# The S5 branch's products and lower parts of the weights: from GpSimd to VectorE

## The chip, the core and the metric

The kernel runs on one core of a Trainium2 chip. The metric is the device time of one execution in microseconds, taken in several runs; the median is given with its range. A profile is one further execution with the hardware profiler on. In its rows PE is TensorE (PEld its weight loads), DVE is VectorE, ACT is ScalarE, POOL is GpSimd and SP is SyncE, which here only issues DMAs.

## What is computed

Two blocks in a row on 512 positions of width 1024: first a mixer of three branches with a squared-ReLU MLP, then a transformer-like layer with a gated delta rule, a Fourier mix and a mixture of experts. The change touches the first block's mixer, cut here to its parts:

```python
proj = jnp.einsum('bsd,de->bse', xn, w_in) + b_in
u_ssm, c_bgate, c_cgate, c_val, g_ssm, g_conv = jnp.split(proj, SPLIT_POINTS, axis=-1)
y_ssm = s5_branch(u_ssm, lam_re, lam_im, log_dt, b_re, b_im, c_re, c_im, d_skip)
z = jax.nn.gelu(y_ssm)
y_a = (z @ w_glu_a) * jax.nn.sigmoid(z @ w_glu_b)
y_b = (c_bgate * causal_short_conv(c_cgate * c_val, conv_w, conv_b)) @ w_conv_out
merged = jax.nn.sigmoid(g_ssm) * y_a + jax.nn.sigmoid(g_conv) * y_b
```

`s5_branch` is a diagonal state space model: 32 groups of 64 complex states, each a linear recurrence over the 512 positions, s[t] = a·s[t−1] + (B u)[t], and y = Re(C s) + d·u.

## The kernel before

**Matmuls in three passes.** Weights and activations are fp32; TensorE is fed a rounded form (fp32r), and each product is made of three: upper weight × upper activation, upper weight × lower activation, lower weight × upper activation. `weights` loads a 1024x256 piece of a weight by a DMA on SP's queue and cuts it into two chunks of 128 columns: ScalarE rounds a chunk to its upper part wh (L125), and the engine named by `self.lsub` subtracts to get the lower part wl (L126), each 128x1024, in two buffers each. `acc3` then runs 16 matmuls with wh (L130 and L131 in turn, the first two passes) and 8 with wl (L138, the third) into one of three PSUM tiles `acc`. `dense` walks over the chunks, hands each finished tile to a function that consumes it, and after each chunk lets the S5 branch go on by `fill` pieces.

**The S5 branch.** `s5` is a generator of 16 steps, each for 128 complex states (one per partition) over all 512 positions. A step has three pieces. First the phase: VectorE makes fr (L442, L445, L446), ScalarE sine sn, absolute value and cosine cs (L448 to L450), TensorE the two input products bu (L455). Then VectorE turns bu back by the phase (L460 to L465) and runs two real scans (L468, L469) that give zr and zi. Then the result is turned forward: sr = cs·zr − sn·zi and si = cs·zi + sn·zr. Here VectorE takes the products with cs (L473, L476), the difference (L475) and the sum (L478); GpSimd takes the two products with sn, n1 (L474) and n2 (L477). After every fourth step TensorE forms y from four sr and four si (L486), and VectorE, ScalarE and VectorE again make z and its two parts (L490, L491, L152, L153).

**The stage.** While S5 runs, TensorE works on 24 chunks of w_in for the convolution branch (its gates and values are consumed by VectorE and ScalarE at L541 to L557), 8 chunks of w_conv_out, and then 8 chunks of w_in for the gate of that branch (L571, L572). With `self.lsub = nc.gpsimd` in `block1` all these 40 chunks' lower parts are made on GpSimd. Behind the gate `lsub` is VectorE again, and z enters the next matmuls.

**What sets the order.** The instructions are laid out on each engine's queue by a scheduler when the program is built, from the order of the code and an estimate of durations. Each engine then takes its queue strictly in order and waits on semaphores, so what stands behind a waiting instruction waits as well.

Of the kernel before, what the change touches and what calls it, by code (L numbers as in the profile page):

```python
# [84 lines left out]
class Kern:  # L85
# [342 lines left out]

    def s5(self, sp, u, zH, zL):
        nc = self.nc  # L430
        V, G = nc.vector, nc.gpsimd
        S = [P, T]

        def t(tag, bufs=1):
            return sp.tile(S, F32, tag=tag, bufs=bufs, name=self.nm(tag))

        st = {}
        for j in range(16):

            fr = t("fr")  # L440
            n = t("m1")
            V.tensor_tensor(fr.rearrange("p (a b) -> p a b", b=16),  # L442
                            self.fa[:, j, :32].unsqueeze(2).broadcast_to([P, 32, 16]),
                            self.fa[:, j, 32:].unsqueeze(1).broadcast_to([P, 32, 16]), op=ALU.add)
            V.tensor_scalar(n, fr, MAGIC, MAGIC, op0=ALU.add, op1=ALU.subtract)  # L445
            V.tensor_sub(fr, fr, n)  # L446
            sn, cs = t("sn", 2), t("cs", 2)
            nc.scalar.activation(sn, fr, AF.Sin, scale=2 * math.pi * (1 - 2e-7))  # L448
            nc.scalar.activation(fr, fr, AF.Abs)
            nc.scalar.activation(cs, fr, AF.Sin, scale=-2 * math.pi, bias=self.halfpi)  # L450
            jr = slice(32 * (j % 4), 32 * (j % 4) + 32)
            bu = []
            for i in range(2):
                b = self.pp.tile(S, F32, tag="q", bufs=4, name=self.nm("bu"))
                nc.tensor.matmul(b, self.bbT[jr, i, j // 4], u[jr, j // 4], start=True, stop=True,  # L455
                                 tile_position=(32 * (j % 4), 0))
                bu.append(b)
            yield
            m1, m2, m3, m4 = t("m1"), t("m2"), t("m3"), t("m4")
            V.tensor_mul(m1, cs, bu[0])  # L460
            V.tensor_mul(m4, sn, bu[0])
            V.tensor_mul(m2, sn, bu[1])
            V.tensor_mul(m3, cs, bu[1])
            V.tensor_add(m1, m1, m2)
            V.tensor_sub(m3, m3, m4)  # L465
            zr, zi = m2, m4
            mg = self.mag[:, j:j + 1].broadcast_to(S)
            V.tensor_tensor_scan(zr, mg, m1, 0.0, op0=ALU.mult, op1=ALU.add)  # L468
            V.tensor_tensor_scan(zi, mg, m3, 0.0, op0=ALU.mult, op1=ALU.add)  # L469
            yield  # L470
            sr, si = t("sr", 4), t("si", 4)
            n1, n2 = m1, m3
            V.tensor_mul(sr, cs, zr)  # L473
            G.tensor_mul(n1, sn, zi)  # L474
            V.tensor_sub(sr, sr, n1)  # L475
            V.tensor_mul(si, cs, zi)  # L476
            G.tensor_mul(n2, sn, zr)  # L477
            V.tensor_add(si, si, n2)  # L478
            st[j % 4] = (sr, si)
            if j % 4 == 3:  # L480
                i4 = j // 4
                y = self.pp.tile(S, F32, tag="q", bufs=4, name=self.nm("y"))
                for i in range(2):
                    for a in range(4):
                        ja = slice(32 * a, 32 * a + 32)
                        nc.tensor.matmul(y[ja, :], self.ccT[:, i, i4, ja], st[a][i], start=(i == 0), stop=(i == 1),  # L486
                                         tile_position=(0, 32 * a), skip_group_check=True)
                ys = t("m1")
                z = t("m2")
                V.scalar_tensor_tensor(ys, u[:, i4], self.v["ssm_d"][:, i4:i4 + 1], y, op0=ALU.mult, op1=ALU.add)  # L490
                nc.scalar.activation(z, ys, AF.Gelu_apprx_tanh)  # L491
                self.split(z, zH[:, i4], zL[:, i4])
            yield

    def block1(self):
        nc, ins = self.nc, self.ins
        V, A = nc.vector, nc.scalar
# [24 lines left out]
        sp = self.pool("s5", es=es)  # L522
        zz = a2.tile([P, 2, 4, T], F32R, tag="Z", name="zz")
        zH, zL = zz[:, 0], zz[:, 1]
        self.lsub = nc.gpsimd
        self.fillers.append(self.s5(sp, u, zH, zL))

        cH = ap_.tile(B, F32R, tag="D", name="cH")
# [105 lines left out]
        zr = tp.tile([P, D], F32, name="zr")  # L634
# [1508 lines left out]
```

## Time and profile before

| | |
|---|---|
| time, median of 3 runs | 1989.0 us (1984.17 to 1991.39) |
| the profiled execution's own time | 1987.15 us |
| its span, first to last instruction | 1985.4 us |
| busy over the whole span: TensorE, VectorE, ScalarE, GpSimd | 1765.2, 1114.9, 585.3, 321.8 us |
| S5 steps, first phase sum to last S5 sum | 79 to 393 us |
| last third pass of the gate's chunks | 432 to 434 us |

The busy times are of the whole kernel, whose stages have different limits; they don't tell what this stage waits for. For that one reads the stretch from 79 to 395 us by itself: how full each engine is in it, which groups of instructions are long for their size, and what lies beside them on the other engines.

### The profile page before, as it was taken

How to read it: one execution, taken by the hardware profiler on the slowest of the kernel's cores; microseconds unless marked ns; L12 is line 12 of the kernel's file. 1: busy time of each engine (PE TensorE's matmuls, PEld its weight loads, DVE VectorE, ACT ScalarE, POOL GpSimd, SP SyncE). 2: the span in 40 equal slices, each digit the busy share in tenths (PEclk: the TensorE clock that was granted, in tenths of full speed). 3: DMA queues.
4: the chain of work that ended last, by engine and by line, in shares of the span. 5: the costliest groups of instructions: out<-in, count | busy, mean ns of one | idle time of the engine just before them, and what ended most of it. 6: DMA issues, size and time to landing. Idle time of an engine off the chain costs nothing. (4 is left out here: it accounts for less than half of the span.)

```text
span 1985.4 us, 24482 instructions
## 1 busy us (share of the span) xinstructions
PE 1765.2 (89%) x9169; PEld 1143.1 (58%) x9169; DVE 1114.9 (56%) x2231; ACT 585.3 (29%) x989; POOL 321.8 (16%) x210
## 2 busy tenths in 40 slices
PE   6778889699999999999998988999698898899985
PEld 4545556376676788777775665887333333333332
DVE  4889898833454665594466689573532323233225
ACT  3222324242343244332344633233411111111112
POOL 0434344420000000000012222003110111111000
PEclk9888889799999999999998889899799999999997
DMA  4111111138556333222231211006599999989993
GB/s 137 63 64 43 43 64 64 42 126 280 210 170 242 120 95 115 67 86 85 64 105 65 64 43 56 13 12 245 206 382 413 413 402 413 389 309 413 412 406 136
DMA packets 150266, 351.15 MB, mean 177 GB/s; under 512 B 20435, under 2 KB 107036, under 8 KB 130235
## 3 DMA queue, kind: packets, MB, share of 16 engines
q1 hardware_dynamic: 135533, 302.52, 41.2%
q0 software_dynamic: 9008, 33.58, 4.6%
q10 hardware_dynamic: 5534, 12.54, 1.7%
q8 instruction: 115, 1.88, 0.4%
q14 instruction: 76, 0.62, 0.1%
HBM read 339.63 MB, written 19.15 MB: 181 GB/s over the span
## 5 line engine op out<-in xcount | busy, mean ns | idle before, releaser
L125 ACT CAST wh<-w 128x1024 fp32r<-128x1024 f32 (+1 forms) x184 | 179.3, 975 | 407.7 <-PE acc L131 340.2
L126 POOL TENSOR_TENSOR wl<-w,wh 128x1024 fp32r<-128x1024 f32 (+1 forms) x76 | 184.7, 2434 | 621.0 <-PE acc L138 375.7
L1733 PE MATMUL gu<-ew,moe 128*64 128x512 f32 x1024 | 262.5, 639 | 14.2 <-DMA ew<-in_w_gate_dram 8.7
L126 DVE TENSOR_TENSOR wl<-w,wh 128x1024 fp32r<-128x1024 f32 (+1 forms) x108 | 123.2, 1141 | 118.7 <-PE acc L138 89.2
L1733 PEld LDWEIGHTS gu<-ew,moe 128*64 128x64 f32 x1024 | 73.9, 145 | 147.8 <-issue 120.4
L130 PE MATMUL acc<-xH,wh 128*128 128x512 f32 x352 | 151.3, 430 | 0.3 <-ACT wh L125 0.3
L131 PE MATMUL acc<-xL,wh 128*128 128x512 f32 x352 | 148.0, 420 | 0.0
L1742 DVE TENSOR_TENSOR moe<-gu,moe 64x512 f32<-64x512 f32 x32 | 21.8, 683 | 201.7 <-ACT moe L1741 136.2
L1758 PE MATMUL dn<-ew,hT 128*64 128x512 f32 x512 | 119.0, 608 | 0.5 <-ACT hT L1751 0.5
L130 PE MATMUL acc<-fH,wh 128*128 128x512 f32 x256 | 103.5, 405 | 0.4 <-ACT fH L152 0.4
L130 PE MATMUL acc<-gH,wh 128*128 128x512 f32 x256 | 103.2, 403 | 0.0
L1751 ACT COPY hT<-tr 128x128 f32<-128x128 f32 x64 | 13.9, 269 | 299.1 <-PE tr L1748 283.3
L131 PE MATMUL acc<-fL,wh 128*128 128x512 f32 x256 | 102.0, 398 | 0.0
L131 PE MATMUL acc<-gL,wh 128*128 128x512 f32 x256 | 102.0, 398 | 0.0
L138 PE MATMUL acc<-xH,wl 128*128 128x512 f32 x352 | 94.4, 412 | 6.5 <-DVE wl L126 3.7
L130 PEld LDWEIGHTS acc<-xH,wh 128*128 128x128 f32 x352 | 71.7, 204 | 42.3 <-issue 19.4
L1703 POOL DMA_INDIRECT yd<-moe,sx x31 | 32.0, 1033 | 339.2 <-DVE moe L1766 168.9
L131 PEld LDWEIGHTS acc<-xL,wh 128*128 128x128 f32 x352 | 71.5, 203 | 21.1 <-issue 5.5
L138 PEld LDWEIGHTS acc<-xH,wl 128*128 128x128 f32 x352 | 69.0, 197 | 24.0 <-DVE wl L126 4.2
L1758 PEld LDWEIGHTS dn<-ew,hT 128*64 128x64 f32 x512 | 36.4, 139 | 68.7 <-issue 63.8
L1766 DVE SCALAR_TENSOR_TENSOR moe<-dn,wv,moe 128x512 f32<-128x512 f32 x32 | 24.0, 751 | 89.5 <-PE dn L1758 64.6
L130 PE MATMUL acc<-hxH,wh 128*128 128x512 f32 x160 | 70.9, 447 | 2.1 <-DVE y L1248 2.1
(706 smaller groups left out, 3458.7 us busy)
## 6 DMA issues: line engine op xcount, KB each, us to landing
ew<-in_w_up_dram SPq DMA_DIRECT2D x64, 1024.0 KB
ew<-in_w_gate_dram SPq DMA_DIRECT2D x64, 1024.0 KB
ew<-in_w_down_dram SPq DMA_DIRECT2D x64, 1024.0 KB
w<-in_w_in_dram SPq DMA_DIRECT2D x36, 1024.0 KB
w<-in_w_ff_dram SPq DMA_DIRECT2D x32, 1024.0 KB
wm<-in_w_mod_dram POOLq DMA_DIRECT2D x24, 1024.0 KB, 6.5
xt<-in_x_dram SPq DMA_DIRECT2D x8, 512.0 KB
w<-in_w_conv_out_dram SPq DMA_DIRECT2D x4, 1024.0 KB
```

The lines of the kernel that those rows point to most:

```text
L125: nc.scalar.copy(H[:, :kt], W[:, :kt, c:c + P])
L126: self.lsub.tensor_sub(L[:, :kt], W[:, :kt, c:c + P], f(H[:, :kt]))
L130: self.nc.tensor.matmul(ps, H[:, k], aH[:, k, sl], start=(k == 0), stop=False)
L131: self.nc.tensor.matmul(ps, H[:, k], aL[:, k, sl], start=False, stop=False)
L138: nc.tensor.matmul(ps, L[:, k], aH[:, k, sl], start=False, stop=(k == kt - 1))
L1703: nc.gpsimd.indirect_dma_start(out=self.yd.rearrange("r (m c) -> (r m) c", m=m), out_offset=bass.IndirectOffsetOnAxis(ap=sx, axis=0), in_= ...
L1733: mm = M.matmul(gu[64 * j:64 * j + 64], xs[:, k, s0:s0 + 64], ws[2 * (k // 4) + j][:, k % 4], start=(n == 0), stop=(n == 7), tile_position ...
L1742: V.tensor_mul(gh[:64], gu[:64], gh[64:])
L1751: put(hT[:, q:q + 2], pt[:, 64 * q:64 * q + 128].rearrange("p (k s) -> p k s", k=2))
L1758: M.matmul(dn[64 * j:64 * j + 64], hT[:, q], ws[4 + q // 2][:, q % 2, 512 * j:512 * j + 512], start=(q == 0), stop=(q == 3), tile_position ...
L1766: V.scalar_tensor_tensor(y, dn, wsl, m5, op0=ALU.mult, op1=ALU.mult)
```

## The change

Three edits. In `s5` the two products with sn go to VectorE (`V` in place of `G`). In `block1` the line that sets `self.lsub` to GpSimd for the S5 stage is gone, so that it stays VectorE, as `setup` set it. Since one line is missing, all lines from 525 on are one lower in the program of after (L549 of before is L548 of after).

```diff
 def s5(self, sp, u, zH, zL):
     nc = self.nc
-    V, G = nc.vector, nc.gpsimd
+    V = nc.vector
...
     V.tensor_mul(sr, cs, zr)
-    G.tensor_mul(n1, sn, zi)
+    V.tensor_mul(n1, sn, zi)
     V.tensor_sub(sr, sr, n1)
     V.tensor_mul(si, cs, zi)
-    G.tensor_mul(n2, sn, zr)
+    V.tensor_mul(n2, sn, zr)
     V.tensor_add(si, si, n2)
...
 sp = self.pool("s5", es=es)
 zz = a2.tile([P, 2, 4, T], F32R, tag="Z", name="zz")
 zH, zL = zz[:, 0], zz[:, 1]
-self.lsub = nc.gpsimd
 self.fillers.append(self.s5(sp, u, zH, zL))
```

The scheduler then lays out the queues anew, from the S5 preparation to the end of the gate; the rows of the later stages stand in the order they had. Three places, with tiles named by the program (m is the tag of the step's four work tiles; the numbers tell instances apart).

VectorE, the tenth S5 step, from the phase to the first products with sine and cosine. Before:

```order
L442 TENSOR_TENSOR fr_1470<-fa 128x512
L445 TENSOR_SCALAR m_263_1471<-fr_1470 128x512
L446 TENSOR_TENSOR fr_1470<-fr_1470,m_263_1471 128x512
L462 TENSOR_TENSOR m_273_1519<-sn_1475,bu_1482 128x512
L460 TENSOR_TENSOR m_272_1518<-cs_1476,bu_1480 128x512
```

The same place after:

```order
L445 TENSOR_SCALAR m_263_1471<-fr_1470 128x512
L556 SCALAR_TENSOR_TENSOR cc_1458<-acc_1534,vt,cc_1458 128x512
L446 TENSOR_TENSOR fr_1470<-fr_1470,m_263_1471 128x512
L126 TENSOR_TENSOR wl_1573<-w_1570,wh_1572 128x1024
L462 TENSOR_TENSOR m_273_1519<-sn_1475,bu_1482 128x512
L153 TENSOR_TENSOR cL<-cc_1458,cH 128x512
L126 TENSOR_TENSOR wl_1630<-w_1570,wh_1629 128x1024
L460 TENSOR_TENSOR m_272_1518<-cs_1476,bu_1480 128x512
```

Two lower parts, which stood on GpSimd's queue, now stand between the phase and the product with the cosine.

VectorE, the end of the same step, where sr and si are formed. Before:

```order
L473 TENSOR_TENSOR sr_1562<-cs_1476,m_273_1519 128x512
L476 TENSOR_TENSOR si_1563<-cs_1476,m_275_1521 128x512
L475 TENSOR_TENSOR sr_1562<-sr_1562,m_272_1518 128x512
L478 TENSOR_TENSOR si_1563<-si_1563,m_274_1520 128x512
L442 TENSOR_TENSOR fr_1603<-fa 128x512
```

The same place after:

```order
L473 TENSOR_TENSOR sr_1562<-cs_1476,m_273_1519 128x512
L474 TENSOR_TENSOR m_272_1518<-sn_1475,m_275_1521 128x512
L476 TENSOR_TENSOR si_1563<-cs_1476,m_275_1521 128x512
L475 TENSOR_TENSOR sr_1562<-sr_1562,m_272_1518 128x512
L477 TENSOR_TENSOR m_274_1520<-sn_1475,m_273_1519 128x512
L442 TENSOR_TENSOR fr_1603<-fa 128x512
L478 TENSOR_TENSOR si_1563<-si_1563,m_274_1520 128x512
```

The products n1 (L474) and n2 (L477) stand among the others, and the next step's phase sum (L442) is drawn ahead of the last sum.

TensorE, the two chunks 1251 and 1304 of one load, at the third pass of the first. Before:

```order
L138 MATMUL acc_1251<-xH,wl_1248 128x512 x8
L455 MATMUL bu_1296<-u,bbT 128x512
L455 MATMUL bu_1298<-u,bbT 128x512
L130 MATMUL acc_1304<-xH,wh_1300 128x512
L131 MATMUL acc_1304<-xL,wh_1300 128x512
```

The third passes of the same two chunks after:

```order
L130 MATMUL acc_1304<-xH,wh_1300 128x512
L131 MATMUL acc_1304<-xL,wh_1300 128x512
L138 MATMUL acc_1251<-xH,wl_1248 128x512 x8
L138 MATMUL acc_1304<-xH,wl_1301 128x512 x8
L486 MATMUL y_1351<-sr_1077,ccT 32x512
L486 MATMUL y_1351<-sr_1145,ccT 32x512
```

The first chunk's third pass moved behind all the matmuls with the second chunk's upper part, so that both third passes stand together.

## Rows read from the trace of the kernel before

**Rows 1.** The page's first line: span and instructions.

```profile
span 1985.4 us, 24482 instructions
```

**Rows 2.** Busy time by stretch: stretch, length, PE, PEld, DVE, ACT, POOL, PEclk, DMA, GB/s.

```profile
79.00:395.00 316.00, 254.21 (x882) 163.11 (x880) 284.16 (x296) 89.43 (x118) 137.49 (x64) 0.86 0.16 54
395.00:434.00 39.00, 39.00 (x162) 31.37 (x163) 13.53 (x10) 17.22 (x20) 14.10 (x8) 0.97 0.30 109
434.00:560.00 126.00, 125.07 (x600) 86.28 (x599) 49.16 (x73) 42.30 (x61) 8.40 (x15) 1.00 0.66 234
```

**Rows 3.** VectorE's groups, 79 to 395 us: busy us, mean ns | idle before.

```profile
L478 DVE TENSOR_TENSOR si<-si,m 128x512 f32<-128x512 f32 x16 | 39.1, 2442 | 0.0
L475 DVE TENSOR_TENSOR sr<-sr,m 128x512 f32<-128x512 f32 x16 | 28.2, 1760 | 1.2 <-POOL m L474 1.2
L476 DVE TENSOR_TENSOR si<-cs,m 128x512 f32<-128x512 f32 x16 | 27.2, 1701 | 0.0
...
L460 DVE TENSOR_TENSOR m<-cs,bu 128x512 f32<-128x512 f32 x16 | 10.9, 683 | 9.4 <-ACT cs L450 9.3
```

**Rows 4.** VectorE's timeline: start us, duration us, instruction, [idle before].

```profile
99.86 0.41 DVE L445 TENSOR_SCALAR m<-fr 128x512 f32<-128x512 f32 x1
100.19 0.54 DVE L549 TENSOR_SCALAR cc<-vp,vt 128x512 f32<-128x512 f32 x1
100.65 0.68 DVE L446 TENSOR_TENSOR fr<-fr,m 128x512 f32<-128x512 f32 x1
101.25 0.74 DVE L550 SCALAR_TENSOR_TENSOR cc<-vp,vt,cc 128x512 f32<-128x512 f32 x1
101.92 0.74 DVE L547 SCALAR_TENSOR_TENSOR vp<-acc,vt,cg 128x512 f32<-128x512 f32 x1
...
106.83 1.21 DVE L468 TENSOR_TENSOR_SCAN m<-magk,m 128x512 f32<-128x512 f32 x1
107.97 1.19 DVE L469 TENSOR_TENSOR_SCAN m<-magk,m 128x512 f32<-128x512 f32 x1
...
313.80 0.68 DVE L478 TENSOR_TENSOR si<-si,m 128x512 f32<-128x512 f32 x1
```

**Rows 5.** GpSimd's timeline, one S5 step, and where it idled later.

```profile
129.44 1.53 POOL L474 TENSOR_TENSOR m<-sn,m 128x512 f32<-128x512 f32 x1 [11.14 <-DVE m L469]
130.94 1.70 POOL L477 TENSOR_TENSOR m<-sn,m 128x512 f32<-128x512 f32 x1
132.60 2.78 POOL L126 TENSOR_TENSOR wl<-w,wh 128x1024 fp32r<-128x1024 f32 x1
...
320.23 5.34 POOL L126 TENSOR_TENSOR wl<-w,wh 128x1024 fp32r<-128x1024 f32 x2 [6.90 <-ACT m L491]
```

**Rows 6.** VectorE's timeline beside the same step.

```profile
129.77 1.75 DVE L476 TENSOR_TENSOR si<-cs,m 128x512 f32<-128x512 f32 x1
131.44 1.74 DVE L475 TENSOR_TENSOR sr<-sr,m 128x512 f32<-128x512 f32 x1
133.11 2.82 DVE L478 TENSOR_TENSOR si<-si,m 128x512 f32<-128x512 f32 x1
135.86 0.68 DVE L153 TENSOR_TENSOR cL<-cc,cH 128x512 fp32r<-128x512 f32 x1
```

**Rows 7.** VectorE's timeline at a lower part that it makes itself.

```profile
41.03 1.22 DVE L126 TENSOR_TENSOR wl<-w,wh 128x1024 fp32r<-128x1024 f32 x1
42.17 0.17 DVE L207 SCALAR_TENSOR_TENSOR dt<-dt,er 128x16 f32<-128x16 f32 x1
```

**Rows 8.** Waits of TensorE, 60 to 430 us: total us, times, longest.

```profile
PE y L486 <- DVE sr L475: 27.2, 7, 7.6
...
PE acc L138 <- POOL wl L126: 2.7, 1, 2.7
```

**Rows 9.** TensorE's timeline in the gate: third passes of two chunks.

```profile
403.89 2.03 PE L138 MATMUL acc<-xH,wl 128*128 128x512 f32 x8
...
409.51 2.03 PE L138 MATMUL acc<-xH,wl 128*128 128x512 f32 x8
```

## The prediction

> **What bounds the kernel now.** I read the stretches first, then the groups of one engine, then the timeline of two engines side by side, and last the waits. The S5 steps run from 79 us (first phase sum, L442) to about 393 us (last L478). Between 79 and 395 us VectorE is busy 284.16 of 316 us, TensorE 254.21 at a granted clock of 0.86 of full speed (a mix of the two levels 1.2 and 2.4 GHz), GpSimd 137.49 with 64 instructions, ScalarE 89.43 [rows 2]. So VectorE is the fullest engine and idles only 316 − 284 = 32 us; 9.4 us of that are waits for the cosine of the step [rows 3].
>
> But VectorE's busy time isn't all its own work. The groups L476, L475 and L478 have means of 1.70, 1.76 and 2.44 us for 128x512 elements, while L460, of the same size but with one of its inputs in PSUM, takes 0.68 us in the mean of its sixteen [rows 3]. The timelines say why: GpSimd runs n1, n2 and a lower part wl back to back from 129.44 to 135.38 us [rows 5], and each VectorE instruction that lies beside it ends just after the GpSimd instruction that started before it: si (L476) runs until 131.52, sr (L475) until 133.18, si (L478) until 135.93. With GpSimd done, the next sum takes 0.68 us again [rows 6]. In a step in which GpSimd then idled, from 313.3 to 320.2 us, L478 took 0.68 us too, at 313.80 [rows 4, 5]. The two engines take turns here, and what GpSimd does costs VectorE nearly as much time as it costs GpSimd.
>
> Behind VectorE stands TensorE: it waited 27.2 us for sr before the y products, and only 2.7 us for a lower part from GpSimd [rows 8]. From 395 us on the last seven chunks of the gate run with TensorE busy 39.00 of 39 us, and so it stays until 560 us (125.07 of 126) [rows 2]: what the S5 stretch gains, TensorE starts earlier by, and nothing in that stage holds it.
>
> **The change, part by part.** Clean prices, from start to start of rows that follow each other without a gap [rows 4]: a 128x512 sum or product 0.60 us, a one-input form (L445, L549) 0.33 to 0.46, a fused form (L550) 0.67, a scan (L468) 1.14. A 128x1024 lower part on VectorE takes 1.14 us, from 41.03 to 42.17 us [rows 7].
>
> *Removed: the turns.* In the stretch VectorE has 296 instructions [rows 2]. By kind, counted in the program: 204 sums, products and splits at 0.60 = 122.4; 16 + 8 one-input forms = 9.0; 32 scans = 36.5; 35 fused forms = 23.5; one copy. Together 191 us. It was busy 284, so 93 us are stretching. Three groups carry most of it: 27.2 + 28.2 + 39.1 − 48 × 0.60 = 65.7 us [rows 3]. With no arithmetic on GpSimd all 93 us go.
>
> *Added to VectorE.* 32 products × 0.60 = 19.2 us, and the 30 lower parts that now stand between the first phase sum and the last L478: 30 × 1.14 = 34.2 us. Sum 53.4 us. VectorE's work in the stretch becomes 191 + 53 = 244 us, 40 less than its 284.
>
> *The idle time of VectorE.* Before, 32 us. Two things move it. In most steps the lower parts now stand between the phase (L446) and the first uses of sine and cosine (L462, L460), so they fill some of those 9.4 us. Against that, a lower part waits in VectorE's queue for its upper part from ScalarE, and for TensorE's third pass to free the buffer of two chunks before; behind it stand the S5 products and with them y on TensorE. Before, GpSimd could wait there alone. That wait has no row of its own: its bounds are 9 us less (the cosine waits all covered) and 30 us more (1 us for each of the 30). I take it as cancelling and keep 32 us, since the filled waits are rows and the new ones fall where ScalarE is busy only 89 of 316 us. Stretch: 244 + 32 = 276 us, 40 less than 316.
>
> *TensorE as the next.* It has 254 us of busy time in the stretch at clock 0.86, so 276 leaves it 22 us of idle time where it had 62. At full speed a chunk takes 5.62 us (403.89 to 409.51 us, third pass to third pass) [rows 9]; the 31 chunks of the stretch need 174 us of it, so part of the 254 is the lower clock after waits, and some comes back. TensorE's order changes too: the third passes of two chunks now stand together behind both chunks' first passes, which gives a late lower part some 4 us more before TensorE waits for it.
>
> *After the stretch.* The last y products stand one chunk earlier in TensorE's order: half a third pass and seven whole chunks follow, where before nine matmuls, one third pass and six chunks followed. That is about 2.5 us more behind the last S5 step, and as much less before it, when TensorE isn't last: +2 us. VectorE's eight lower parts there cost 1.14 us in a cycle of 5.62 and are hidden by TensorE. *Before the stretch* four lower parts move from GpSimd: between −4 × (2.78 − 1.14) = −6.6 and +4 × 1.14 = +4.6 us; I take −1, since GpSimd's stretch the preparation in the same way. *GpSimd's queue:* the DMAs of the modulation weights no longer stand behind lower parts and may start earlier, with DMA at 0.16 of its capacity in the stretch [rows 2]: 0.
>
> Sum: −40 + 2 − 1 = −39, say −40 us. The profiled execution took 1987.15 us, 1.75 more than its span of 1985.4 [rows 1], and lies 1.85 below the median of 1989.0. 1987 − 40 = **1947 us**.
>
> **A rule that speaks against it.** VectorE is busy 0.90 of the stretch and GpSimd 0.44 [rows 2]. The Trainium skill, "Perfetto Trace Analysis", section "Optimizing Scalar/DVE Operations", says that where VectorE is saturated it may make sense to hand some work to GpSimd; the change does the opposite. The same passage adds that the two share a read port of SBUF, so that moving work between them might not help. By the first half the time would be that of rival C, by the second that of the sum; rows 5 and 6 show the turns, so I go by the second.
>
> **The rivals.**
> *A, TensorE holds the stretch back.* If TensorE keeps its 254 us at clock 0.86 and half or more of its 62 us of waits, because y still stands behind sr and si in its order, the stretch is 285 to 301 us, the gain 15 to 31 and the time 1956 to 1972. For it: VectorE's work (244) is now below TensorE's busy time (254). Against: the waits for sr shrink with VectorE, and the clock rises when waits go.
> *B, the waits shrink too.* If the lower parts cover the cosine waits and TensorE is always ahead, VectorE idles 12 to 20 us: stretch 256 to 264, time 1927 to 1935. For it: the places of the lower parts in the order. Against: TensorE would have to run nearly without a wait.
> *C, slower.* If the long L475, L476 and L478 were not due to GpSimd, VectorE would keep its 284 us and get 53 more: stretch 337 + 32 = 369, time 2040. It decides from 53 us of stretching that stays, of the 93. Against: L478 at 0.68 us where GpSimd was idle [rows 4, 5].
> *D, given back later.* If the modulation weights or a later stage started at a fixed time, the gain would be lost behind 434 us and the time 1980 to 1990. Against: TensorE is full there [rows 2], and the order of the program behind the gate is unchanged.
> That the change doesn't do what it says is out: the new program has no arithmetic on GpSimd between the S5 preparation and the modulation.
>
> **How the numbers follow.** The forecast with idle time between 22 and 42 us, 1937 to 1957: 0.50. A beyond it, up to 1972: 0.25. B, 1927 to 1937: 0.14. C: 0.04. D: 0.05. Anything else: 0.02. The range takes in the forecast and most of A and B: 1930 to 1970, about 0.82. A measurement of this kernel can tell about 0.5% (10 us) from no change: faster 0.90 (forecast, A, B and a little), same 0.06, slower 0.04.
>
> **What would show it.** L475, L476 and L478 at 0.68 us in all sixteen steps, n1 and n2 at 0.68 and lower parts at about 1.2 us on VectorE; VectorE busy about 244 us from the first L442 to the last L478, and that stretch 270 to 285 us long; TensorE's waits for sr below 27 us and a clock over 0.86. Wrong would be: VectorE's instructions still stretched (C); VectorE idle over 50 us with waits for TensorE (A); the gate beginning 40 us earlier and the end not (D).

## The result: faster, by half as much again as forecast

The changed kernel takes 1929.54 us in the median of 4 runs (1923.76 to 1932.94), the kernel before 1990.2 on the same chip: a ratio of 0.9693, 95% interval 0.9654 to 0.9732. A second measurement beside other runs gave 1927.88 (0.9689, 0.9661 to 0.9716). The gain is 61 us where 40 were forecast, and the time lies just outside the stated range of 1930 to 1970. The profiled execution of the changed kernel took 1923.76 us, 1921.9 of it span; it was the shortest of its runs.

Busy time of the changed kernel by stretch, in the columns of [rows 2] (stretch, length, PE, PEld, DVE, ACT, POOL, PEclk, DMA, GB/s): the S5 steps, the rest of the gate, and as much behind it as the third row of [rows 2] has:

```profile
77.00:336.00 259.00, 233.00 (x859) 154.63 (x858) 245.35 (x357) 87.37 (x114) 0.00 (x0) 0.93 0.18 61
336.00:378.00 42.00, 42.00 (x178) 32.88 (x177) 14.08 (x19) 18.56 (x23) 2.01 (x3) 1.00 0.37 127
378.00:504.00 126.00, 124.37 (x597) 85.79 (x596) 49.14 (x73) 41.78 (x61) 8.39 (x15) 1.00 0.66 232
```

The first row of [rows 2] ends 2 us behind the last S5 sum. Cut there, the S5 steps of the kernel before are:

```profile
79.00:393.00 314.00, 252.27 (x879) 162.83 (x877) 283.55 (x296) 89.43 (x118) 137.49 (x64) 0.87 0.17 54
```

The S5 steps last 259 us where they lasted 314. Of these 55 us, VectorE is busy 38 less, though it executes 61 instructions more, and it idles 17 less: 259 − 245 = 14 us where it idled 314 − 284 = 30. TensorE is full again from there on, as in [rows 2]. VectorE's groups in the first stretch, in the columns of [rows 3]:

```profile
L126 DVE TENSOR_TENSOR wl<-w,wh 128x1024 fp32r<-128x1024 f32 x30 | 36.4, 1216 | 1.2 <-PE acc L138 1.2
...
L460 DVE TENSOR_TENSOR m<-cs,bu 128x512 f32<-128x512 f32 x16 | 10.9, 683 | 3.2 <-ACT cs L450 3.1
L462 DVE TENSOR_TENSOR m<-sn,bu 128x512 f32<-128x512 f32 x16 | 10.9, 682 | 2.1 <-ACT sn L448 2.1
...
L476 DVE TENSOR_TENSOR si<-cs,m 128x512 f32<-128x512 f32 x16 | 10.9, 682 | 0.0
...
L475 DVE TENSOR_TENSOR sr<-sr,m 128x512 f32<-128x512 f32 x16 | 10.9, 681 | 0.0
L478 DVE TENSOR_TENSOR si<-si,m 128x512 f32<-128x512 f32 x16 | 10.9, 681 | 0.0
```

The three long groups of [rows 3] are at 0.68 us. The wait for the cosine at L460 has gone from 9.4 to 3.2 us. Its neighbour, the wait for the sine, stood one row further in the same view of the kernel before:

```profile
L462 DVE TENSOR_TENSOR m<-sn,bu 128x512 f32<-128x512 f32 x16 | 10.9, 683 | 6.8 <-ACT sn L448 5.9 <-PE acc L131 0.7
```

Why these waits shrank is seen in VectorE's timeline of the changed kernel (start us, duration us, instruction):

```profile
126.68 0.68 DVE L446 TENSOR_TENSOR fr<-fr,m 128x512 f32<-128x512 f32 x1
127.28 1.22 DVE L126 TENSOR_TENSOR wl<-w,wh 128x1024 fp32r<-128x1024 f32 x1
128.45 0.69 DVE L462 TENSOR_TENSOR m<-sn,bu 128x512 f32<-128x512 f32 x1
129.06 1.22 DVE L126 TENSOR_TENSOR wl<-w,wh 128x1024 fp32r<-128x1024 f32 x1
130.32 0.69 DVE L460 TENSOR_TENSOR m<-cs,bu 128x512 f32<-128x512 f32 x1
```

From the end of the phase (L446) ScalarE needs some microseconds for sine, absolute value and cosine. Two lower parts now lie in that time, and VectorE goes from one product to the next without a pause. Twelve of the sixteen steps have one or two lower parts there, 17 of the 30 in all. Of the 5.3 us of waits that are left, 2.8 are those of the first step, which has none.

One reading of the forecast turned round: TensorE no longer waits much for sr, but it waits for lower parts. Its waits from 60 to 375 us in the changed kernel (total us, times, longest), against 27.2 and 2.7 us in [rows 8]:

```profile
PE acc L138 <- DVE wl L126: 19.2, 5, 8.8
PE y L486 <- DVE sr L475: 5.5, 3, 4.7
```

What these waits cost by themselves isn't shown. It is TensorE that ends the stage: it is busy without a pause from the last S5 sum to the gate's last third pass. From the first phase sum to there, before and after:

```profile
79.00:434.00 355.00, 293.21 (x1043) 194.47 (x1042) 297.69 (x306) 106.65 (x138) 151.59 (x72) 0.88 0.18 60
77.00:378.00 301.00, 275.00 (x1036) 187.51 (x1035) 259.44 (x375) 105.92 (x136) 2.01 (x3) 0.94 0.21 70
```

Its matmuls are nearly the same (1043 and 1036 records). The 54 us are 36 us less idle time of TensorE (62 to 26) and 18 us less busy time, at a mean granted clock of 0.94 in place of 0.88 (mixes of its two levels, 1.2 and 2.4 GHz). The shorter chain on VectorE pays by what TensorE no longer waits for.

### The profile page after: what moved, and what is told of

The parts are those of the page before. It is cut to its first block, busy times and chain, and to the rows that moved or that the text cites. A ratio compares the mean times of both kernels' runs of the same rounds, so it can differ in the third digit from the quotient of the medians.

```text
span 1921.9 us, 24414 instructions
## 1 busy us (share of the span) xinstructions
PE 1746.7 (91%) x9169; PEld 1134.6 (59%) x9169; DVE 1074.8 (56%) x2303; ACT 585.9 (30%) x988; POOL 162.5 (8%) x138
## 5 line engine op out<-in xcount | busy, mean ns | idle before, releaser
L126 DVE TENSOR_TENSOR wl<-w,wh 128x1024 fp32r<-128x1024 f32 (+1 forms) x148 | 171.8, 1162 | 139.7 <-PE acc L138 100.9
L130 PE MATMUL acc<-xH,wh 128*128 128x512 f32 x352 | 145.0, 412 | 0.0
L131 PE MATMUL acc<-xL,wh 128*128 128x512 f32 x352 | 141.7, 402 | 0.0
L138 PE MATMUL acc<-xH,wl 128*128 128x512 f32 x352 | 101.1, 435 | 23.8 <-DVE wl L126 23.8
L126 POOL TENSOR_TENSOR wl<-w,wh 128x1024 fp32r<-128x1024 f32 (+1 forms) x36 | 78.5, 2185 | 456.6 <-PE acc L138 308.9
L130 PE MATMUL acc<-fH,wh 128*128 128x512 f32 x256 | 103.7, 406 | 0.4 <-ACT fH L152 0.4
L130 PE MATMUL acc<-gH,wh 128*128 128x512 f32 x256 | 103.2, 403 | 0.0
L138 PEld LDWEIGHTS acc<-xH,wl 128*128 128x128 f32 x352 | 72.9, 211 | 48.0 <-DVE wl L126 28.2
L130 PEld LDWEIGHTS acc<-xH,wh 128*128 128x128 f32 x352 | 67.7, 192 | 35.3 <-issue 12.0
L131 PEld LDWEIGHTS acc<-xL,wh 128*128 128x128 f32 x352 | 67.5, 192 | 17.8 <-issue 3.2
L130 PE MATMUL acc<-hxH,wh 128*128 128x512 f32 x160 | 71.6, 452 | 2.1 <-DVE y L1247 2.1
L131 PE MATMUL acc<-hxL,wh 128*128 128x512 f32 x160 | 68.6, 433 | 0.0
```

The lines of the kernel that those rows point to most:

```text
L126: self.lsub.tensor_sub(L[:, :kt], W[:, :kt, c:c + P], f(H[:, :kt]))
L130: self.nc.tensor.matmul(ps, H[:, k], aH[:, k, sl], start=(k == 0), stop=False)
L131: self.nc.tensor.matmul(ps, H[:, k], aL[:, k, sl], start=False, stop=False)
L138: nc.tensor.matmul(ps, L[:, k], aH[:, k, sl], start=False, stop=(k == kt - 1))
```

## The experiments

The theory of the forecast is that VectorE and GpSimd take turns, so that GpSimd's work costs VectorE most of its length. For the idle time, which fell by 17 us where the forecast kept it, there are two theories: **1**, the lower parts on VectorE's queue fill the waits for sine and cosine; **2**, the turns themselves made the idle time. In the runs "the gate's end" is the first matmul with z (L130 with zz; L137 in e6), at 433.9 us in the kernel before and 377.7 in the changed one. Ratios are to the kernel before on the same chip. The edits of e1 and e2 stand against the kernel before, that of e8 and e9 is the same on either kernel, and the others stand against the changed kernel.

### Only the products (e1)

```diff
-            G.tensor_mul(n1, sn, zi)
+            V.tensor_mul(n1, sn, zi)
...
-            G.tensor_mul(n2, sn, zr)
+            V.tensor_mul(n2, sn, zr)
```

> Only the two products of each S5 step go to VectorE; the lower parts stay on GpSimd. Both theories take VectorE's work from 191 us (all clean) to 191 + 19 = 210, plus turns with the 32 lower parts, 85.6 of GpSimd's 137.5 us, so about 58 of the 93 us of stretching: 268 us from the first phase sum to the last S5 sum. Theory 1 (the lower parts on VectorE's queue fill its waits for sine and cosine, which is why its idle time fell from 30 to 14 us): none stand there in this kernel, the waits for sine and cosine stay at 15 us, the idle time about 30, the stretch 298, the time 1990 - 16 = 1974. Theory 2 (the turns themselves made the idle time, products and lower parts alike): idle about 20 us, stretch 288, time 1964.

Measured: 1957.83 us, ratio 0.9827 (0.981 to 0.9843). The S5 steps last 299 us, the length of theory 1, but in part by luck: VectorE is busy 260 us where 268 were expected, and idles 39 where 30 were:

```profile
81.00:380.00 299.00, 265.02 (x960) 175.29 (x958) 259.87 (x331) 101.09 (x128) 99.75 (x35) 0.92 0.19 62
```

and VectorE's groups in it have the two waits whole:

```profile
L462 DVE TENSOR_TENSOR m<-sn,bu 128x512 f32<-128x512 f32 x16 | 10.9, 684 | 11.8 <-ACT sn L448 11.6
L460 DVE TENSOR_TENSOR m<-cs,bu 128x512 f32<-128x512 f32 x16 | 10.9, 683 | 17.6 <-ACT cs L450 17.5
```

They are 29 us, more than the 15 expected and than the kernel before had. They did not shrink with the products' turns, and theory 2, which had an idle time of 20 us, is out. What made them longer is in part ScalarE's queue. In the last step the sigmoid of a gate chunk (L571) stands there between sine and cosine, with loads of function tables of 1.28 us each, and VectorE waits twice:

```profile
362.48 0.69 DVE L462 TENSOR_TENSOR m<-sn,bu 128x512 f32<-128x512 f32 x1 [3.65 <-ACT sn L448]
368.18 0.69 DVE L460 TENSOR_TENSOR m<-cs,bu 128x512 f32<-128x512 f32 x1 [3.02 <-ACT cs L450]
```

But the time is 16 us below theory 1's: the new order draws some three chunks of the gate into the stretch (960 matmul records where [rows 2] has 882), and the gate ends 22 us after the last S5 step where the kernel before needed 41. A stretch is thus not the time; the gate's end, here 401.4 us, is.

### Only the lower parts (e2)

```diff
-        self.lsub = nc.gpsimd
```

> Only the lower parts go to VectorE; the two products of each step stay on GpSimd. VectorE's work: 191 + 30 x 1.14 = 225 us, plus turns with the 32 products, 53 of GpSimd's 137.5 us, so about 36 us: 261. Theory 1 (the lower parts fill the waits for sine and cosine): these waits fall to about 5 us as in the changed kernel, idle time about 14 us, stretch 275, time 1990 - 39 = 1951. Theory 2 (the turns made the idle time): idle about 24 us, stretch 285, time 1961.

Measured: 1954.24 us, ratio 0.982 (0.9802 to 0.9838). The S5 steps last 277.7 us, near theory 1's 275, and the gate ends at 401.3. The length alone doesn't decide between the theories, since VectorE is busy 8 us less than expected and idles 24 us, which is theory 2's figure:

```profile
77.00:354.00 277.00, 233.07 (x844) 154.60 (x847) 252.75 (x323) 86.78 (x113) 52.57 (x32) 0.92 0.17 57
```

The waits decide. VectorE's groups from 77 to 354 us:

```profile
L475 DVE TENSOR_TENSOR sr<-sr,m 128x512 f32<-128x512 f32 x16 | 27.0, 1688 | 7.1 <-POOL m L474 7.1
L476 DVE TENSOR_TENSOR si<-cs,m 128x512 f32<-128x512 f32 x16 | 21.9, 1366 | 0.0
L460 DVE TENSOR_TENSOR m<-cs,bu 128x512 f32<-128x512 f32 x16 | 10.9, 683 | 3.2 <-ACT cs L450 2.9
L462 DVE TENSOR_TENSOR m<-sn,bu 128x512 f32<-128x512 f32 x16 | 10.9, 679 | 2.1 <-ACT sn L448 2.1
```

With lower parts in VectorE's queue the waits for sine and cosine are 5 us, with the turns of the products still there (L475, L476), as theory 1 has it. The rest of the 24 us are other waits: 7 us for GpSimd's products (L475), and some 12 for TensorE and at the lower parts. Each half of the change moves the gate's end by 32.5 us, both together by 56. The halves don't add up. TensorE's idle time up to the gate's end, 62 us before and 26 in the changed kernel, is 34 us with the products alone and 44 with the lower parts alone; why the two overlap isn't shown.

### The products once more, for nobody (e3)

```diff
             V.tensor_add(si, si, n2)
+            g1, g2 = t("g1"), t("g2")
+            nc.gpsimd.tensor_mul(g1, sn, zi)
+            nc.gpsimd.tensor_mul(g2, sn, zr)
```

> The changed kernel, and GpSimd takes the two products of each step once more into tiles that nobody reads (32 products, about 52 us of GpSimd). Theory of the turns: VectorE's instructions beside them are stretched by about 0.68 of that, 35 us, and the time is about 1930 + 35 = 1965, though nobody waits for GpSimd. Rival (the long instructions before came from waiting for GpSimd's results or buffers, not from its work): no change, 1930, all VectorE means as in the changed kernel.

Measured: 1963.75 us, ratio 0.9861 (0.9839 to 0.9883): 34 us above the first measurement of the changed kernel, as the turns would have it. No engine waits for these products in the trace, yet two of VectorE's groups are long again (from 76 to 368 us):

```profile
L474 DVE TENSOR_TENSOR m<-sn,m 128x512 f32<-128x512 f32 x16 | 28.2, 1765 | 0.0
L473 DVE TENSOR_TENSOR sr<-cs,m 128x512 f32<-128x512 f32 x16 | 26.7, 1669 | 0.0
```

GpSimd's 32 products take 59 us, and VectorE's busy time is 279.3 us, 34 more than in the changed kernel. This shows the mechanism by itself: it needs no wait for a result or a buffer of GpSimd's.

### Zeros in place of products (e4)

```diff
+        g1 = sp.tile([P, D], F32, name="g1")
+        for _ in range(240):
+            nc.gpsimd.memset(g1, 0.0)
         self.fillers.append(self.s5(sp, u, zH, zL))
```

> The changed kernel, and GpSimd writes zeros into one tile without a pause, 240 times 128x1024, some 230 us from the start of the S5 steps on. Theory (VectorE and GpSimd take turns only where GpSimd reads): no change, 1930, VectorE's two-input instructions at 0.68 us. Rival (any arithmetic instruction of GpSimd makes VectorE wait): VectorE is stretched by some 0.68 x 230 = 156 us, time about 2086.

Measured: 1933.54 us, ratio 0.9702 (0.9683 to 0.972), with GpSimd busy 231 of the 263 us of the S5 steps. VectorE's groups in them (L551 is the first tap of the convolution, L548 in the changed kernel):

```profile
L475 DVE TENSOR_TENSOR sr<-sr,m 128x512 f32<-128x512 f32 x16 | 10.9, 681 | 0.0
L478 DVE TENSOR_TENSOR si<-si,m 128x512 f32<-128x512 f32 x16 | 10.9, 680 | 0.0
L445 DVE TENSOR_SCALAR m<-fr 128x512 f32<-128x512 f32 x16 | 10.7, 672 | 0.0
L551 DVE TENSOR_SCALAR cc<-vp,vt 128x512 f32<-128x512 f32 x8 | 8.1, 1017 | 0.0
```

The instructions with two tensors don't feel a GpSimd that only writes. The two one-input forms do: 0.67 and 1.02 us in the mean, where the changed kernel has 0.42 and 0.54. Together that is 10.7 + 8.1 − 6.7 − 4.3 = 7.8 us. The Trainium skill, "SBUF — State Buffer", section "Who interferes with whom", says the same: a VectorE instruction with two inputs in SBUF contends with a GpSimd instruction that reads SBUF and not with one that only writes it, while one-input forms can enter a mode that takes both of VectorE's ports and contends with GpSimd. This run agrees with the part on writes (two-input instructions at 0.68 us), and with the last part in that the one-input forms grew longer; which mode they were in it doesn't show.

### The changed kernel again (e5)

The kernel is the changed one, without an edit.

> The changed kernel once more, on the chip of the runs beside it. Time 1930; the gate's last third pass at 378 us as in the first profile. If the 5 us that the profile gained behind the gate belong to the change, the stretch from the gate's end to the first gather of the experts is 985 us again and the rest 559; if they are chance, both move by some microseconds.

Measured: 1927.88 us. The gate ends at 375.3 us, 2.4 earlier than in the first profile; from there to the first gather of the experts it takes 989.0 us (985.1 in the first profile of this kernel, 987.2 in the kernel before), and from the gather to the end 563.9 (559.1 and 564.3). Behind the gate the first profile had gained 7 us of the 63.5 between the two spans; here the same program loses 1 us there. So those 7 us are not shown to be the change's; the 56 to 59 us at the gate's end are.

### No lower parts at all (e6)

The weights' own lower parts of the S5 stage are left out; all third passes take one lower part that is made once.

```diff
+            nc.scalar.copy(H[:, :kt], W[:, :kt, c:c + P])
+            if self.nolow:
+                if self.L0 is None:
+                    self.L0 = self.a2.tile([P, 8, P], F32R, tag="L0", name="L0")
+                    self.lsub.tensor_sub(self.L0, W[:, :, c:c + P], f(H))
+                yield H, self.L0
+                continue
             L = self.wp.tile([P, 8, P], F32R, tag="wl", bufs=2, name=self.nm("wl"))
-            nc.scalar.copy(H[:, :kt], W[:, :kt, c:c + P])
...
+        self.nolow = True
         self.fillers.append(self.s5(sp, u, zH, zL))
...
         self.lsub = nc.vector
+        self.nolow = False
```

> The changed kernel without the lower parts of the S5 stage: the third passes all take one lower part, made once (the weights' own lower parts of 39 chunks are left out, the matmuls are all there). VectorE's work falls by 30 x 1.14 to 211 us. Theory 1 (the lower parts on VectorE's queue fill the waits for sine and cosine): with none there these waits grow from 5 us to 15 or more. Theory 2 (the waits shrank because GpSimd's turns went): they stay at 5 us. The S5 part then ends with TensorE, whose busy time of 233 us is the floor: stretch 235 to 245 us, time 1910 to 1920.

Measured: 1897.16 us, ratio 0.9535 (0.9509 to 0.9562), 31 us below the changed kernel on the same chip and more than expected. VectorE's groups from 75 to 321 us, where L467 and L469 are the lines L460 and L462:

```profile
L467 DVE TENSOR_TENSOR m<-cs,bu 128x512 f32<-128x512 f32 x16 | 11.0, 687 | 12.2 <-ACT cs L457 12.1
L469 DVE TENSOR_TENSOR m<-sn,bu 128x512 f32<-128x512 f32 x16 | 11.0, 685 | 8.6 <-ACT sn L455 8.5
```

With no lower parts there, and nothing on GpSimd either, the waits for sine and cosine are 21 us again: theory 1 is shown from the other side. TensorE is then the fuller engine (238.57 of 246 us, at a clock of 0.98), so VectorE has little more to give there. The 31 us, 26 of them at the gate's end (349.0 us), are what making the lower parts on VectorE still costs, TensorE's waits for them included.

### The second block's lower parts (e7 and e11)

```diff
-        self.lsub = Q
```

> The changed kernel, and the 36 lower parts of the second block's x path (L126 on GpSimd, 78.5 us there) go to VectorE too. Theory of the turns: VectorE's work there rises by 20 x 1.14 + 16 x 0.60 = 32 us and falls by up to 0.68 x 78 = 53; VectorE is fullest from 1100 to 1200 us (0.91). Gain 0 to 15 us, time 1915 to 1930. Rival: VectorE's queue then holds back the matmuls, which wait there for it: 5 to 15 us slower.

Measured: 1922.21 us, ratio 0.9654 (0.962 to 0.9687). The same kernel once more:

> The kernel of e7 again, in more rounds: 1922 if its 6 us below the changed kernel were real, 1929 if they were chance.

Measured: 1924.57 us, ratio 0.9658 (0.9638 to 0.9679). Both lie 3 to 6 us below the changed kernel, but the intervals overlap with its 0.9661 to 0.9716: likely a small gain, not settled. From the gate's end to the first gather the two profiles take 981.6 and 978.9 us, where the changed kernel took 985.1 and 989.0, which speaks for the gain. The turns are there too: the costliest group of VectorE between 1100 and 1200 us (a fused form) takes 0.91 us in the mean in e5 and 0.74 in e7. What limits that stage along its length wasn't tested.

### The phase one step ahead (e8 and e9)

The same edit on both kernels: the phase (L442 to L450) becomes a function that is called for the next step behind the scans' inputs, with its scratch n in a tile of its own.

```diff
-        for j in range(16):
-
+        def phase(j):
             fr = t("fr")
-            n = t("m1")
+            n = t("n")
...
+            return sn, cs
+
+        ph = phase(0)
+        for j in range(16):
+            sn, cs = ph
...
             V.tensor_sub(m3, m3, m4)
+            if j < 15:
+                ph = phase(j + 1)
             zr, zi = m2, m4
```

On the kernel before:

> The kernel before, all of GpSimd's work in place, but each step's phase (L442 to L450) is made one step ahead, behind the scans, so that sine and cosine are ready. If VectorE's waits for sine and cosine (15 us of its 30 us of idle time) are time on the path, the stretch falls from 314 to about 299 us and the time to 1975. If they only cover waits that come anyway (for TensorE, or GpSimd's turns), the time stays at 1990.

Measured: 1969.76 us, ratio 0.9908 (0.9879 to 0.9936), 20 us faster with GpSimd's work as it was. The waits for sine and cosine fell from 15 to 3 us, the S5 steps from 314 to 289, the gate's end to 415.2. From 80 to 369 us:

```profile
80.00:369.00 289.00, 232.79 (x841) 154.18 (x843) 273.99 (x294) 88.09 (x115) 136.21 (x63) 0.89 0.17 55
```

So there were two ways to shorten those waits: other work in the gap, as the change did, or the phase earlier. But they make up 12 of the 25 us only. VectorE is also busy 9 us less, with as much work on GpSimd: the new order changed what lies beside it. That the waits alone were worth 20 us isn't shown. In VectorE's groups of that run the waits are (L466 and L464 are the lines L462 and L460):

```profile
L466 DVE TENSOR_TENSOR m<-sn,bu 128x512 f32<-128x512 f32 x16 | 10.8, 676 | 2.0 <-ACT sn L447 2.0
...
L464 DVE TENSOR_TENSOR m<-cs,bu 128x512 f32<-128x512 f32 x16 | 10.8, 674 | 3.5 <-PE bu L459 2.8 <-ACT cs L449 0.7
```

On the changed kernel:

> The changed kernel with each step's phase made one step ahead. In the kernel before that was worth 20 us. If what it gave there were the waits for sine and cosine, only 5 us of them are left here: time 1930 - 5 = 1925. If it helps TensorE as well (y and the input products earlier), up to 15 us more. If it costs, because the phase displaces the scans on VectorE's queue, the time is above 1930.

Measured: 1941.11 us, ratio 0.9762 (0.9736 to 0.9788), 12 to 13 us slower than the changed kernel. The gain that the expectation put first, 5 us, had the wrong sign; it allowed for a cost, but by another cause. The waits for sine and cosine are 3 us, but VectorE now waits longer for TensorE, which has done less by then in the new order of the queues. From 77 to 340 us:

```profile
L562 DVE SCALAR_TENSOR_TENSOR cc<-acc,vt,cc 128x512 f32<-128x512 f32 x8 | 5.9, 742 | 4.4 <-PE acc L138 4.4
L552 DVE SCALAR_TENSOR_TENSOR vp<-acc,vt,cg 128x512 f32<-128x512 f32 x8 | 5.9, 739 | 4.3 <-PE acc L138 4.3
L496 DVE SCALAR_TENSOR_TENSOR m<-u,vt,y 128x512 f32<-128x512 f32 x3 | 2.2, 747 | 5.1 <-PE y L492 5.1
```

and more of the gate is left behind the last S5 step: 821 matmul records lie in the S5 steps in place of 860, and from the last S5 sum it takes 48 us in place of 42, the gate's end at 388.0.

### Put together (e10 and e12)

> The changed kernel with the phase one step ahead, no lower parts on GpSimd in the second block either, and the first tap of the convolution (8 instructions of 0.46 us) on ScalarE. Gains if they add up: 5 us, 6 us (as e7 measured) and 4 us: time 1930 - 15 = 1915, about 75 us below the kernel before. If the schedule of the new order eats the small ones, 1922 as e7 alone.

Measured: 1924.58 us, ratio 0.9683 (0.9655 to 0.9711): 3 to 5 us below the changed kernel, within the noise, where 15 were expected. The edits are the phase ahead, that of e7 and the first tap of the convolution on ScalarE. Without the phase ahead, that is the kernel of e7 with one more edit:

```diff
-                V.tensor_scalar(c, vp[:, 2:], cw[:, 16 + ch:17 + ch], cb[:, ch:ch + 1], op0=ALU.mult, op1=ALU.add)
+                A.activation(c, vp[:, 2:], AF.Identity, scale=cw[:, 16 + ch:17 + ch], bias=cb[:, ch:ch + 1])
```

> e7 with the first tap of the convolution on ScalarE (8 instructions of 0.46 us off VectorE, of its 245 us in the S5 part): 1918 to 1920 if VectorE's work alone sets the S5 part, 1922 or more if the new order of the queues moves the waits instead, as it did with the phase one step ahead.

Measured: 1911.51 us, ratio 0.9601 (0.9577 to 0.9626), the best kernel with the whole computation, 16 to 18 us below the changed one and 79 below the kernel before. It differs from e10 by the phase alone, which thus costs some 13 us here, as it did in e9. Its profile accounts for 5 us of the gain at the gate's end (372.6 us). But the profiled execution, with a span of 1921.1 us, was longer than four of the six timed runs (1907 to 1912 us), so where the rest lies isn't seen and stays open.

## Why the forecast was wrong

- **The turns.** Right. All sixteen of L475, L476 and L478 are at 0.68 us, and e3 shows the turns with nobody waiting. VectorE's work was forecast as 244 us and measured as 245.35. This step carried 38 of the 61 us.
- **The prices of the added work.** Right: the lower parts on VectorE take 1.216 us a record and the products 0.68, as the rows had it.
- **The idle time of VectorE.** This is the step that failed: "I take it as cancelling and keep 32 us". It is 14, and the 17 us by which it fell are nearly all of what the forecast lacked. Two things were weighed wrongly. I set the gain's bound at the 9 us of the cosine waits and left out the sine's row beside it, 6.8 us; both fell, to 5 us together. And I set 30 us of new waits against it, 1 us for each lower part, with no row behind the price: the lower parts waited 1.2 us in all. The order of the changed program, which stood ahead of the forecast, already showed the lower parts in the gap; e1, e2 and e6 show that this is what filled it: 29, 5 and 21 us of those waits without, with and without lower parts on VectorE's queue. These waits are 10 of the 17 us. The others were not tested: the wait for the gelu (L445, 3.5 us before) is gone, the one for GpSimd's product (L475, 1.2) as well, and those for TensorE fell from 10 to 8 us.
- **TensorE as the next.** The 4 us more that a late lower part was to have did not keep TensorE from waiting: it waits 19.2 us for them. It had the room, because its clock rose from 0.86 to 0.93 and its busy time in the stretch fell from 254 to 233 us; about 5 us of that fall are 23 matmul records that now lie behind the stretch. Rival A, which took the 254 as fixed, is out.
- **Before and after the stretch.** The first phase sum is 2 us earlier (−1 forecast), and from the last S5 sum to the gate's end it takes 41.7 us instead of 40.9 (+2 forecast).
- **Rivals.** B held: idle 12 to 20 us, 1927 to 1935, with a chance of 0.14. Its second condition, TensorE always ahead, was not met: VectorE still waits 8 us for TensorE, and TensorE itself idles 26. C is out: the long groups are short without GpSimd's work, and e3 makes others long with it. Of the rule that the prediction draws from the Trainium skill, "Perfetto Trace Analysis", section "Optimizing Scalar/DVE Operations", the half that speaks for handing work to GpSimd did not hold in this stage, and the half that it might not help did. D is out: TensorE is full behind the gate and the gate's 56 us arrive at the end.

## What to carry to other kernels

A group of instructions that is long for its size is the first thing to look for on a full engine, and here the cause lay in the timeline of the engine that runs beside it; an offload that stretches its neighbour's instructions, here by 0.57 (e3) to 0.68 (the forecast's 93 of 137.5 us) of its own length, must save more than that. When work moves onto an in-order queue, look where it lands: in a gap that waits for another engine it costs little there, and such a gap should be priced with the row of every wait in it, not with the largest. And measure a stage by its end, not by the length of one chain in it: e1 shortened the S5 steps by 15 us and the gate's end came 32 earlier, e9 lengthened them by 3 and it came 10 later, because the scheduler also moved the work around them.

## What the runs showed of the hardware

GpSimd instructions that read hold VectorE's instructions with two inputs in SBUF, and ones that only write do not: 32 products for nobody cost 34 us, 231 us of zeros left all of those at their length. Zeros did stretch VectorE's one-input forms, in the mean from 0.42 to 0.67 and from 0.54 to 1.02 us, which I had not expected. And instructions with one input in PSUM (L460 to L463) stayed at 0.68 us beside GpSimd's lower parts too: some 3 of L460's 16 lay beside one in the kernel before and 8 in e1, and none took more than 0.69 us.
